# First layer's queries and keys: three matmuls of 256 columns per weight block against one of 512 and one of 256

## The chip, the core and the metric

The kernel runs on one core of a Trainium2 chip. The time is that of one execution on the device, in microseconds (us), as the median of several runs. TensorE multiplies matrices into the banks of PSUM, VectorE and ScalarE do elementwise work, GpSimd a few small things, and SyncE starts the transfers from memory. The profile calls TensorE's matmuls PE and its weight loads PEld, VectorE DVE, ScalarE ACT, GpSimd POOL and SyncE SP.

## What is computed

Two layers of an encoder over 256 tokens with 1024 features, in float32. The first layer mixes tokens in two ways at once: eight heads of attention over a neighbourhood on a grid, and eight heads of attention over compressed latents. Both start from one input projection and end in one output projection. The second layer has three groups of dilated windows. An MLP with a squared ReLU follows each. This is the part that the change touches:

```python
def even_mixer(xn, w_in, rpb, q_norm, w_uq, kv_norm, w_ukv, w_o, cos_r, sin_r):
    hcat = xn @ w_in
    o0 = 3 * NA_WIDTH                      # 1536: queries, keys and values of 8 heads of 64
    a_qkv = hcat[..., :o0].reshape(b, s, 3, NA_HEADS, HEAD_DIM)
    out_a = neighbourhood_attention(a_qkv[:, :, 0], a_qkv[:, :, 1], a_qkv[:, :, 2], rpb)
    c_q = rms_norm(hcat[..., o0:o1], q_norm)
    c_kv = rms_norm(hcat[..., o1:o2], kv_norm)
    ...
    out_b = dense_attention(q, k, v, (MLA_NOPE + MLA_ROPE) ** -0.5)
    return jnp.concatenate([out_a, out_b], axis=-1) @ w_o

for layer in range(DEPTH):
    xn = rms_norm(x, norm_mix[layer])
    x = x + even_mixer(xn, ...) if layer % 2 == 0 else x + odd_mixer(xn, ...)
    x = x + sq_relu_mlp(rms_norm(x, norm_mlp[layer]), mlp_w1[layer], mlp_w2[layer])
```

## The kernel before

**Two parts of every number.** The matmuls take a shortened form of float32. To keep precision, each operand is held as two tensors: the rounded value ("high") and what is left of it ("low"). A product is the sum of three matmuls: high times high, high times low, low times high. The helper `mm3` (L185 to L187) does that, always into the same part of one bank. The helper `split` makes the two parts: ScalarE rounds (L181), VectorE subtracts (L182).

**The tokens.** `pair_tile` holds both parts of the normalised tokens beside each other, as 8 row blocks of 2 times 256 columns: `xh` is the high part of a block, `xl` the low part, `xp` both as one stretch of 512 columns. The MLP (L370, L371) and the second layer's queries and keys (L867, L868) use `xp`: one matmul of 512 columns puts the high weight times both parts into the two halves of a bank, a second of 256 adds the low weight times the high part to the first half, and when the bank is emptied the halves are added.

**The weights.** They come from memory in chunks of 2048 columns, in the order of a list. `weight()` hands out the next chunk and sends for later ones: loads run four chunks ahead, splits two.

**The first layer's row of work.** First comes a part whose order is written out by hand (latents and values, L533 and around). Then come four chunks of queries and keys, one for each pair of heads (`qk_steps`, L621 and below). A chunk is four steps: feature half f = 0 (queries) and 1 (keys), each in two halves of four row blocks, with one `mm3` per row block. Both feature halves go into one bank, half and half. After the last step VectorE multiplies the bank by `both` (L636), which holds the tokens' scales, and `split` gives `qk_h` and `qk_l`, from which the scores of two heads are made.

The list `main` holds these steps of chunks 1 to 3, then the latent projections (`uq_steps`, `ukv_steps`), then three quarters of the output projection. Between them the attention is spread by estimated costs: for each of 16 items a score (L194 for the neighbourhood, `mm3` for the latents), its softmax on VectorE and ScalarE (L728 to L736), four transposes of its probabilities (L743), their copy to SBUF (L745) and the mixture with the values (L757). That is only the order in which the program is written. Outside the part with a hand-written order, the framework's scheduler makes each engine's order from it, by priorities and estimates of its own.

**Banks.** PSUM has eight banks here, four under the name `w` and four under `acc`, handed out in turn. Chunk 0 of queries and keys uses `w`, the others `acc`, as do the mixtures of the first six items and the latent projections. Scores and transposes use `w`. A bank is free again once everything that reads it is done.

Of the kernel before, what the change touches and what calls it, by code (L numbers as in the profile page):

```python
# [19 lines left out]
ALU = mybir.AluOpType  # L20
# [5 lines left out]
KT = D // P  # L26
T = 256
# [19 lines left out]
def trunk(ctx, tc, a, out):  # L47
    nc = tc.nc
# [8 lines left out]
    def scratch(shape, name):  # L57

        n = int(np.prod(shape))
        v = work.tile([P, 512], F32, tag="scratch", name=name, bufs=12)[:, :n]  # L60
        if len(shape) == 2:
            v = v.rearrange("p (a b) -> p a b", b=shape[1])
        return v

    def pair_tile():


        z = act.tile([P, KT, 2, T], F32R, tag="pair", name="pair", bufs=1)
        return z[:, :, 0, :], z[:, :, 1, :], z
# [7 lines left out]
    def bank(tag):  # L77
        return ps.tile([P, 512], F32, tag=tag, name=tag)
# [5 lines left out]
    def load_x(k, n=1):  # L84
        c = slice(4 * KT + k * T if k else 0, 4 * KT + (k + n) * T)
        nc.sync.dma_start(gx[:, c], a["gx"][:, c])
# [56 lines left out]
    def load_weight(edges=None, earlier=lambda i: None):  # L143
        j = state["loaded"]
        src, n = specs[j]
        raw = wraw.tile([P, WCH], F32, tag="raw", name="raw")
        edges = edges or (0, n)
        for i, c in enumerate(slice(*e) for e in zip(edges, edges[1:])):
            earlier(i)
            nc.sync.dma_start(raw[:, c], src[:, c])  # L150
        parts[j] = [raw, None, None]
        state["loaded"] = j + 1
# [13 lines left out]
    def prefetch(loads, splits):  # L166
        while state["loaded"] < min(loads, len(specs)):
            load_weight()
        while state["split"] < min(splits, len(specs)) * WPARTS:
            split_piece()  # L170

    def weight():

        j = state["used"]
        prefetch(j + 1, j + 1)
        prefetch(j + LOAD_AHEAD, j + SPLIT_AHEAD)
        state["used"] = j + 1
        return parts.pop(j)[1:]

    def split(hi, lo, src, eng=None):  # L180
        a = nc.scalar.copy(hi, src).ins  # L181
        return a, (eng or nc.vector).tensor_tensor(lo, src, hi.bitcast(F32), op=ALU.subtract).ins  # L182

    def mm3(o, sh, sl, mh, ml, first, last):
        nc.tensor.matmul(o, sh, mh, start=first, stop=False)  # L185
        nc.tensor.matmul(o, sh, ml, start=False, stop=False)  # L186
        nc.tensor.matmul(o, sl, mh, start=False, stop=last)  # L187
# [27 lines left out]
    def two(z):  # L215
        return z.rearrange("p (f n) -> p f n", f=2)
# [68 lines left out]
    def hand_over(accs, last, n):  # L285

        xT, s = pair_tile(), sum_tile()
        for b in range(4):
            last[b]()
            with tc.high_priority(NORM_PRIO):  # L290
                join(b, accs[b], n, xT)
        return xT, s

    def hand_over_tokens(accs, last, n, scale):

        xT, s = pair_tile(), sum_tile()
        ys = {}

        def leave(h, t):
            last(h, t)  # L300
            acc, sc = accs[2 * t + h], column(scale, t)
            with tc.high_priority(NORM_PRIO):
                y = ys[h, t] = scratch([512], "y")
                nc.scalar.activation(y[:, 0:T], acc[:, 0:T], AF.Copy, scale=sc)
                nc.vector.tensor_scalar(y[:, T:2 * T], acc[:, T:2 * T], sc, None, ALU.mult)

        def turn(h):
            with tc.high_priority(NORM_PRIO):
                for b in range(2):
                    pt = bank("w")  # L310
                    for k in range(2):
                        for t in range(NT):
                            c = (2 * b + k) * P
                            nc.tensor.transpose(pt[:, k * T + t * P:k * T + (t + 1) * P], ys[h, t][:, c:c + P], ident)
                    join(2 * h + b, pt, n, xT)

        leave(0, 0)
        leave(0, 1)
        leave(1, 0)
        turn(0)  # L320
        leave(1, 1)
        turn(1)
        return xT, s
# [166 lines left out]


    def even(ep):
        xT = xh, xl, _ = pair_tile()
        load_weight((0, 416, CV, CV + 416, 2 * CV), lambda i: load_x(i // 2) if i % 2 == 0 else None)
        load_weight((0, CV, 2 * CV), lambda i: load_x(2, 2) if i == 0 else None)
        load_weight((0, 2 * 416, 4 * 416), lambda i: load_x(4 + 2 * i, 2))
        both = ep.tile([P, 2, T], F32, name="both")
# [125 lines left out]
        def qk_steps(c):  # L623
            hold = {}

            def step(f, half):
                if not hold:
                    hold["w"], hold["p"] = weight(), bank("acc" if c else "w")
                (wh, wl), pq = hold["w"], hold["p"]
                for k in range(4 * half, 4 * half + 4):  # L630
                    ws = slice(k * 256 + f * P, k * 256 + f * P + P)
                    mm3(pq[:, f * T:(f + 1) * T], wh[:, ws], wl[:, ws], xh[:, k, :], xl[:, k, :], k == 0, k == KT - 1)
                if f == 1 and half == 1:
                    th, tl = (ep.tile([P, 2, T], F32R, tag=n, name=n, bufs=2) for n in ("qk_h", "qk_l"))
                    q32 = scratch([2, T], "q32")
                    nc.vector.tensor_tensor(q32, pq.rearrange("p (f n) -> p f n", f=2), both, op=ALU.mult)  # L636
                    split(th, tl, q32)
                    qk[c] = th, tl

            return [lambda f=f, h=h: step(f, h) for f in range(2) for h in range(2)]  # L640
# [368 lines left out]
    def phase(name, fn, *args):  # L1009
        with tc.tile_pool(name=name, bufs=1, reuse_waits="tile") as pool:  # L1010
            return fn(pool, *args)

    accs, last = phase("even", even)
    xT, s = hand_over(accs, last, 1)
    accs, last, scale = phase("mlp0", mlp_between, xT, s)
    xT, s = hand_over_tokens(accs, last, 2, scale)
    accs, last = phase("odd", odd, xT, s)
    xT, s = hand_over(accs, last, 3)
# [95 lines left out]
```

## Time and profile before

| | us |
|---|---|
| median of 3 runs | 747.87 |
| lowest, highest | 747.73, 748.14 |
| the profiled execution | 748.65 |
| its span, first to last instruction | 746.9 |
| first matmul of the queries and keys | 26.79 |
| first matmul of the latent projections | 58.36 |
| first matmul of the first MLP | 114.39 |

The three last rows are places in the span. All rows of a profile that follow come from the one profiled execution. A row of a timeline has the start and the length in us, then the engine, the line of the kernel, the operation, the tile written and the tiles read, the shapes and a count. Where a row has a bracket, the engine stood idle before it for that long, and the arrow names what ended the idle time. The granted clock of TensorE was 0.997 of the full one on average.

### The profile page before, as it was taken

The page shows a single profiled execution, that of the slowest core. Times are in us where ns is not written, and L with a number is a line of the kernel's source. Part 1 is how long each engine was busy: PE and PEld are TensorE (multiplying, and loading weights), DVE is VectorE, ACT ScalarE, POOL GpSimd, SP SyncE. Part 2 cuts the span into 40 slices and gives each one's busy share as a digit, 9 for nine tenths or more (in the row PEclk, how much of TensorE's full clock was granted, in tenths as well). Part 3 has the DMA queues.
Part 4 walks back from the last instruction along what each step waited for, and adds up shares of the span by engine and source line. Part 5 has one row for each costly group of instructions (what it writes and reads, how often), then busy time and mean ns, then how long its engine had stood idle before and what let it go on. Part 6 is the DMA issues. An engine that isn't in the chain of part 4 may idle for free.

```text
span 746.9 us, 12279 instructions
## 1 busy us (share of the span) xinstructions
PE 739.0 (99%) x4635; PEld 646.4 (87%) x4635; DVE 544.2 (73%) x1137; ACT 484.8 (65%) x1075; POOL 8.7 (1%) x20
## 2 busy tenths in 40 slices
PE   9999999999999999999999999999999999999996
PEld 6998998888888888889899899998998888888885
DVE  6778858766566666997888788888858765665664
ACT  6788967554554555677786877867856554554551
POOL 0100000000000001000000000000000000000000
PEclk9999999999999999999999999999999999999998
DMA  8763334464555545554645636445545555545501
GB/s 282 317 255 114 114 113 170 171 225 173 179 211 177 186 172 165 200 183 165 208 141 178 223 122 215 165 162 198 203 165 176 190 198 197 186 183 187 193 15 56
DMA packets 25163, 133.19 MB, mean 178 GB/s; under 512 B 3728, under 2 KB 4752, under 8 KB 12304
## 3 DMA queue, kind: packets, MB, share of 16 engines
q1 hardware_dynamic: 24960, 132.15, 50.1%
q8 instruction: 36, 0.59, 0.3%
q10 hardware_dynamic: 144, 0.26, 0.1%
q14 instruction: 23, 0.19, 0.1%
HBM read 127.16 MB, written 1.05 MB: 172 GB/s over the span
## 4 chain that ended last, share of the span: by engine, by line
PE 93%; DMA 3%; DVE 1%; issue 1%; SPq 1%; ACT 1%; POOL 0%; POOLq 0%; ACTq 0%
PE w L370 16%; PE acc L185 14%; PE acc L187 13%; PE acc L186 13%; PE acc L867 12%; PE w L371 8%; PE acc L868 6%; PE w L194 1%; PE w L945 1%; PE w L925 1%; PE w L743 1%; DMA gx<-in_gx 1%; DMA bias<-in_rpb 1%; DMA raw<-in_w_v 1%; PE w L757 1%
## 5 line engine op out<-in xcount | busy, mean ns | idle before, releaser
L182 DVE TENSOR_TENSOR wlo<-raw,whi 128x512 fp32r<-128x512 f32 (+3 forms) x487 | 306.6, 664 | 135.1 <-ACT whi L181 134.4
L181 ACT CAST whi<-raw 128x512 fp32r<-128x512 f32 (+3 forms) x487 | 264.3, 601 | 171.3 <-PE w L370 62.3
L370 PE MATMUL w<-pair,whi 128*128 128x512 f32 x512 | 182.2, 397 | 0.0
L371 PE MATMUL w<-pair,wlo 128*128 128x256 f32 x512 | 143.9, 281 | 0.0
L867 PE MATMUL acc<-pair,whi 128*128 128x512 f32 x384 | 139.4, 403 | 0.0
L370 PEld LDWEIGHTS w<-pair,whi 128*128 128x128 f32 x512 | 96.2, 188 | 23.2
L868 PE MATMUL acc<-pair,wlo 128*128 128x256 f32 x384 | 108.1, 282 | 0.0
L185 PE MATMUL acc<-whi,hh 128*128 128x512 f32 x250 | 98.1, 392 | 0.0
L187 PE MATMUL acc<-whi,hl 128*128 128x512 f32 x250 | 97.7, 391 | 0.0
L186 PE MATMUL acc<-wlo,hh 128*128 128x512 f32 x250 | 97.7, 391 | 0.0
L371 PEld LDWEIGHTS w<-pair,wlo 128*128 128x128 f32 x512 | 96.1, 188 | 0.9
L867 PEld LDWEIGHTS acc<-pair,whi 128*128 128x128 f32 x384 | 72.2, 188 | 16.2
L868 PEld LDWEIGHTS acc<-pair,wlo 128*128 128x128 f32 x384 | 72.2, 188 | 0.2 <-issue 0.2
L187 PEld LDWEIGHTS acc<-whi,hl 128*128 128x128 f32 x250 | 47.0, 188 | 9.9
L185 PEld LDWEIGHTS acc<-whi,hh 128*128 128x128 f32 x250 | 47.0, 188 | 9.8
L186 PEld LDWEIGHTS acc<-wlo,hh 128*128 128x128 f32 x250 | 47.0, 188 | 8.9
L185 PE MATMUL acc<-whi,pair 128*128 128x384 f32 x128 | 43.8, 342 | 0.0
L187 PE MATMUL acc<-whi,pair 128*128 128x384 f32 x128 | 43.1, 337 | 0.0
L186 PE MATMUL acc<-wlo,pair 128*128 128x384 f32 x128 | 43.1, 337 | 0.0
L374 ACT COPY side<-w 128x256 f32<-128x256 f32 x64 | 23.7, 370 | 22.1 <-PE w L371 22.1
L375 DVE TENSOR_TENSOR u<-w,side 128x256 f32<-128x256 f32 x64 | 27.0, 421 | 3.8 <-ACT side L374 3.0
L181 ACT CAST hh<-hsq 128x512 fp32r<-128x512 f32 x32 | 19.9, 621 | 10.2 <-DVE hsq L377 10.2
(215 smaller groups left out, 1112.3 us busy)
## 6 DMA issues: line engine op xcount, KB each, us to landing
raw<-in_w SPq DMA_DIRECT2D x64, 1024.0 KB, 4.8
raw<-in_w_oqk SPq DMA_DIRECT2D x24, 1024.0 KB, 5.0
raw<-in_w_ov SPq DMA_DIRECT2D x16, 768.0 KB, 4.4
raw<-in_w_qk SPq DMA_DIRECT2D x4, 1024.0 KB, 8.9
raw<-in_w_oe SPq DMA_DIRECT2D x4, 1024.0 KB, 5.2
sw<-qk SPq DMA_DIRECT2D x64, 64.0 KB, 2.4
raw<-in_w_oo SPq DMA_DIRECT2D x4, 1024.0 KB, 5.1
bias<-in_rpb SPq DMA_DIRECT2D x8, 256.0 KB, 4.2
```

What stands on the lines that cost most here:

```text
L181: a = nc.scalar.copy(hi, src).ins
L182: return a, (eng or nc.vector).tensor_tensor(lo, src, hi.bitcast(F32), op=ALU.subtract).ins
L185: nc.tensor.matmul(o, sh, mh, start=first, stop=False)
L186: nc.tensor.matmul(o, sh, ml, start=False, stop=False)
L187: nc.tensor.matmul(o, sl, mh, start=False, stop=last)
L194: nc.tensor.matmul(o[j], y[pb, 0, ts], z[pb, 1, :], start=n == 0, stop=n == 2)
L370: nc.tensor.matmul(two(pu[f]), w[0][:, c], xT[2][:, k], start=k == 0, stop=False)
L371: nc.tensor.matmul(pu[f][:, 0:T], w[1][:, c], xT[0][:, k, :], start=False, stop=k == KT - 1)
L374: nc.scalar.copy(side[:, f], pu[f][:, T:2 * T])
L375: nc.vector.tensor_tensor(u[:, f], pu[f][:, 0:T], side[:, f], op=ALU.add)
L867: nc.tensor.matmul(two(pq), wh[:, ws], xp[:, k], start=k == 0, stop=False)
L868: nc.tensor.matmul(pq[:, 0:T], wl[:, ws], xh[:, k, :], start=False, stop=k == KT - 1)
```

## The change

In `qk_steps` the three matmuls of 256 columns give way to one of 512 columns (the high weight with both parts of the tokens) and one of 256 (the low weight with the high part). The 512 columns fill a bank, so each feature half has a bank of its own: two per chunk instead of one. When a feature half is complete, VectorE adds the halves of its bank into `q32` with one TENSOR_REDUCE; after the second one `q32` is multiplied by `both` in place and split as before.

```diff
-        xT = xh, xl, _ = pair_tile()
+        xT = xh, xl, xp = pair_tile()
...
                 if not hold:
-                    hold["w"], hold["p"] = weight(), bank("acc" if c else "w")
-                (wh, wl), pq = hold["w"], hold["p"]
+                    hold["w"], hold["q"] = weight(), scratch([2, T], "q32")
+                if half == 0:
+                    hold["p"] = bank("acc" if c else "w")
+                (wh, wl), pq, q32 = hold["w"], hold["p"], hold["q"]
                 for k in range(4 * half, 4 * half + 4):
                     ws = slice(k * 256 + f * P, k * 256 + f * P + P)
-                    mm3(pq[:, f * T:(f + 1) * T], wh[:, ws], wl[:, ws], xh[:, k, :], xl[:, k, :], k == 0, k == KT - 1)
+                    nc.tensor.matmul(two(pq), wh[:, ws], xp[:, k], start=k == 0, stop=False)
+                    nc.tensor.matmul(pq[:, 0:T], wl[:, ws], xh[:, k, :], start=False, stop=k == KT - 1)
+                if half == 1:
+                    nc.vector.tensor_reduce(q32[:, f], pq.rearrange("p (h n) -> p n h", h=2), axis=mybir.AxisListType.X, op=ALU.add)
                 if f == 1 and half == 1:
...
-                    q32 = scratch([2, T], "q32")
-                    nc.vector.tensor_tensor(q32, pq.rearrange("p (f n) -> p f n", f=2), both, op=ALU.mult)
+                    nc.vector.tensor_tensor(q32, q32, both, op=ALU.mult)
                     split(th, tl, q32)
```

In the changed kernel the two matmuls are L636 and L637, the sum is L639, the multiplication L642, and every line below is six higher than before (the transposes L749, the mixtures L763, the score minimum L734).

The built orders of the two kernels differ from the first query-key matmul to the end of the first layer. Three places follow.

On TensorE, around the score of the third item (its L194 rows; `pp` are probabilities, `qk_h` and `qk_l` the parts of a chunk's queries and keys; "x2" are the two heads), before:

```order
L187 MATMUL acc<-pair,wlo 128x256
L743 MATMUL w<-ident,pp 128x128 x4
L194 MATMUL w<-qk_h 128x256 x2
L194 MATMUL w<-qk_l,qk_h 128x256 x2
L194 MATMUL w<-qk_h,qk_l 128x256 x2
L185 MATMUL acc<-pair,whi 128x256
```

And at the same place in the changed kernel:

```order
L636 MATMUL acc<-pair,whi 128x512
L749 MATMUL w<-ident,pp 128x128 x2
L194 MATMUL w<-qk_h 128x256
L749 MATMUL w<-ident,pp 128x128 x2
L194 MATMUL w<-qk_l,qk_h 128x256
L194 MATMUL w<-qk_h,qk_l 128x256
L637 MATMUL acc<-pair,wlo 128x256
L636 MATMUL acc<-pair,whi 128x512
L637 MATMUL acc<-pair,wlo 128x256
L194 MATMUL w<-qk_h 128x256
L194 MATMUL w<-qk_l,qk_h 128x256
L194 MATMUL w<-qk_h,qk_l 128x256
```

The four transposes and the score stood whole; now the two heads' matmuls stand apart, with transposes and three projections between them. The first item's score is cut in a similar way, by four projections behind its first pass.

On TensorE in the output projection (the rows that read `oah` and `oal`), at a mixture (L757, of `pts` with the values `vml`), before:

```order
L187 MATMUL acc<-oah,wlo 128x256
L743 MATMUL w<-ident,pp 128x128 x4
L757 MATMUL w<-pts,vml 64x128 x4
L185 MATMUL acc<-oah,whi 128x256
```

And in the changed kernel:

```order
L185 MATMUL acc<-oah,whi 128x256
L749 MATMUL w<-ident,pp 128x128 x2
L763 MATMUL w<-pts,vml 64x128
L749 MATMUL w<-ident,pp 128x128 x2
L763 MATMUL w<-pts,vml 64x128 x3
L187 MATMUL acc<-oah,wlo 128x256
```

The transposes and the mixture are cut into each other. That pattern stood at one mixture before and stands at three now.

On VectorE, from the second latent split to the split of chunk 1 (`cl` is a latent's low part, `sn` and `mn` are a score and its minimum), before:

```order
L182 TENSOR_TENSOR cl<-w,ch 128x3x128
L636 TENSOR_TENSOR q_527<-acc,both 128x512
L728 ISA sn,mn<-w,bias 128x256
L728 ISA mn 128x1
L728 ISA sn,mn<-w,bias 128x256
L728 ISA mn 128x1
L182 TENSOR_TENSOR qk_l<-q_527,qk_h 128x512
```

And in the changed kernel:

```order
L182 TENSOR_TENSOR cl<-w,ch 128x3x128
L639 TENSOR_REDUCE q_457<-acc 128x256 x2
L734 ISA sn,mn<-w,bias 128x256
L734 ISA mn 128x1
L642 TENSOR_TENSOR q_457<-q_457,both 128x512
L734 ISA sn,mn<-w,bias 128x256
L734 ISA mn 128x1
L182 TENSOR_TENSOR wlo<-raw,whi 128x512
L182 TENSOR_TENSOR qk_l<-q_457,qk_h 128x512
```

The first minimum stood behind one multiplication and stands behind two sums; the multiplication stands between the two heads' minima.

## The prediction

> **What bounds the kernel now.** I read the page's busy shares and its chain of work first, then the busy time of the two stretches that the change can touch, then who waited for whom on TensorE there.
>
> ```profile
> PE 739.0 (99%) x4635; PEld 646.4 (87%) x4635; DVE 544.2 (73%) x1137; ACT 484.8 (65%) x1075; POOL 8.7 (1%) x20
> ...
> PE 93%; DMA 3%; DVE 1%; issue 1%; SPq 1%; ACT 1%; POOL 0%; POOLq 0%; ACTq 0%
> ```
>
> ```profile
> 26.79:58.36 31.57, 31.39 (x280) 28.92 (x278) 25.19 (x80) 27.08 (x74) 2.14 (x4) 1.00 0.68 251
> 58.36:114.39 56.03, 56.03 (x474) 49.75 (x473) 44.38 (x136) 46.45 (x129) 0.88 (x3) 1.00 0.32 112
> ```
>
> ```profile
> PE w L556 <- DVE cn L548: 0.2, 1, 0.2
> ```
>
> The first stretch runs from the first query-key matmul to the first matmul of the latent projections, the second from there to the first matmul of the MLP. The columns are length, then busy time of TensorE matmuls, weight loads, VectorE, ScalarE and GpSimd, then granted clock, DMA share and GB/s. TensorE is busy for 31.39 of 31.57 us and 56.03 of 56.03, at a granted clock of 1.00, and its one listed wait is 0.2 us. The chain is TensorE's for 93%. So a microsecond more or less in TensorE's row of instructions moves the end by about as much, and VectorE (25.19 of 31.57) matters only where it makes TensorE wait. Because matmul ends are modelled and overlap, I price TensorE from start to start, not by the busy time of one.
>
> **The matmuls themselves.** Before, each of 64 steps (4 weights, 2 feature halves, 8 row blocks) issues three matmuls of 256 columns; after, one of 512 and one of 256. Both are 768 columns. The trace has both forms, on the same moving tile and with weights of the same shape.
>
> ```profile
> 26.79 0.28 PE L185 MATMUL w<-pair,whi 128*128 128x256 f32 x1
> ...
> 30.89 0.61 PE L265 MATMUL w<-diag,mean 128*128 128x128 f32 x4
> ```
>
> ```profile
> 149.77 0.40 PE L370 MATMUL w<-pair,whi 128*128 128x512 f32 x1
> ...
> 154.36 0.39 PE L185 MATMUL acc<-whi,hh 128*128 128x512 f32 x1
> 154.59 0.39 PE L186 MATMUL acc<-wlo,hh 128*128 128x512 f32 x1
> ```
>
> Between the first two rows stand 36 matmuls of 256 (12 steps): (30.89 − 26.79)/36 = 0.114 us each, 0.342 a step. Between 149.77 and 154.36 the MLP does 13 pairs of the new form (26 matmuls): 4.59/13 = 0.353 a step. The new form is 0.0114 us slower, times 64: **+0.7 us**. What it saves, 64 weight loads, is hidden: they lie beside matmuls already.
>
> The Trainium skill, "TensorE: Matmul & The Clock Gate", section "Back-to-back issue gap", gives a warm gap of N/2.4 + 2.5 ns between matmuls standing alone. By it three of 256 take 327.5 ns and a pair 325.0, so the change would gain 64 × 2.5 ns = 0.16 us as an estimate. The trace disagrees: 342 against 353 ns; I go by the trace.
>
> **The order of the row on TensorE.** The built order shows that the change also moves what stands between the projections. Scores (L194), transposes of probabilities (L743) and mixtures (L757) are cut into pieces at places where they stood whole.
>
> ```profile
> 39.11 0.28 PE L187 MATMUL acc<-pair,wlo 128*128 128x256 f32 x1
> 39.31 0.38 PE L194 MATMUL w<-qk_h 64*128 64x256 f32 x2
> 39.54 0.28 PE L194 MATMUL w<-qk_l,qk_h 64*128 64x256 f32 x2
> 39.66 0.28 PE L194 MATMUL w<-qk_h,qk_l 64*128 64x256 f32 x2
> 39.86 0.38 PE L185 MATMUL acc<-pair,whi 128*128 128x256 f32 x1
> 40.09 0.28 PE L186 MATMUL acc<-pair,whi 128*128 128x256 f32 x1
> ```
>
> Going over to a score and back costs: the last projection before it takes 39.31 − 39.11 = 0.20 instead of 0.11, the first behind it 0.23. So one more cut through a score by projections costs 0.20 on the projections, and some 0.1 on the score, whose piece ends with a gap of 0.20 (39.66 to 39.86) where 0.12 stands between its passes. The first score is cut once: **+0.3 us**.
>
> ```profile
> 82.53 0.38 PE L743 MATMUL w<-ident,pp 128*128 128x128 f32 x2
> 82.84 0.43 PE L757 MATMUL w<-pts,vml 128*64 128x128 f32 x2
> 83.20 0.44 PE L743 MATMUL w<-ident,pp 128*128 128x128 f32 x2
> 83.57 0.65 PE L757 MATMUL w<-pts,vml 128*64 128x128 f32 x6
> 84.15 0.39 PE L185 MATMUL w<-kh,qh 96*128 96x256 f32 x1
> ```
>
> ```profile
> 89.91 0.60 PE L743 MATMUL w<-ident,pp 128*128 128x128 f32 x4
> 90.44 0.66 PE L757 MATMUL w<-pts,vml 128*64 128x128 f32 x8
> 91.03 0.39 PE L185 MATMUL acc<-oah,whi 128*128 128x256 f32 x1
> ```
>
> The same four transposes and one mixture take 84.15 − 82.53 = 1.62 us cut into each other and 91.03 − 89.91 = 1.12 whole: a cut of this kind costs 0.50. The third score stood whole behind four transposes; after, its two heads, which ran side by side (rows with x2), stand apart, cut by two transposes and by three projections. By the two rows above that is 0.5 + 0.3: **+0.8 us**. In the output projection the pattern "two transposes, a piece of a mixture, two transposes, the rest" stands three times where it stood once: **+1.0 us**. A mixture in the second stretch is cut 3 to 1 by four transposes, and elsewhere single projections stand between pairs of transposes, while other transposes lose the gap that they have in front of a score (44.84 to 45.37: 0.53) against a projection (55.31 to 55.67: 0.36).
>
> ```profile
> 44.84 0.60 PE L743 MATMUL w<-ident,pp 128*128 128x128 f32 x4
> 45.37 0.39 PE L194 MATMUL w<-qk_h 64*128 64x256 f32 x2
> ...
> 55.31 0.60 PE L743 MATMUL w<-ident,pp 128*128 128x128 f32 x4
> 55.67 0.37 PE L185 MATMUL acc<-pair,whi 128*128 128x256 f32 x1
> ```
>
> These go both ways by 0.17 or so apiece: between −0.3 and +0.3, taken as **0**.
>
> **The idle that goes.** TensorE stands still once in the first stretch, for the normalised latent rows:
>
> ```profile
> 34.31 0.28 PE L187 MATMUL acc<-pair,wlo 128*128 128x256 f32 x1
> 34.77 0.52 PE L556 MATMUL w<-ident,cn 128*128 128x128 f32 x3 [0.18 <-DVE cn L548]
> ```
>
> The gap is 0.46 where 0.11 is normal. After, these transposes stand behind 20.5 steps of 0.353 instead of 20 of 0.342, about 0.4 us later, and VectorE's order up to them is unchanged: the idle of 0.35 us is filled, **−0.35**. What is late next is the first score.
>
> **VectorE.** Eight sums over a bank are added. The odd layer has the same operation:
>
> ```profile
> L876 DVE TENSOR_REDUCE qk<-acc 128x256 f32<-128x512 f32 x24 | 16.5, 686 | 5.1 <-PE acc L868 4.9
> ...
> L636 DVE TENSOR_TENSOR q<-acc,both 128x512 f32<-128x512 f32 x3 | 2.1, 692 | 1.5 <-PE acc L187 1.5
> ```
>
> ```profile
> 310.82 0.69 DVE L876 TENSOR_REDUCE qk<-acc 128x256 f32<-128x512 f32 x1
> 311.43 0.68 DVE L182 TENSOR_TENSOR wlo<-raw,whi 128x512 fp32r<-128x512 f32 x1
> ```
>
> From start to start one takes 0.61 us, eight 4.9; the multiplication by `both` stays, now from SBUF, and keeps its 0.69. VectorE's 25.19 us become about 30.1 in a stretch of some 33: 91%. Behind a sum stand, in VectorE's row, the score minimum (L728), the split of q and k (L182 to qk_l) and weight splits; TensorE waits for these through the softmax and for the split. The first minimum stands behind two sums now, 1.2 us. The cover is the distance from a score to the transposes of its probabilities: the score ends at 39.86, the transposes begin at 44.84, 5.0 us. And VectorE at 91% is already seen without harm:
>
> ```profile
> 58.00:76.00 18.00, 18.00 (x142) 14.92 (x140) 16.46 (x56) 16.42 (x49) 0.88 (x3) 1.00 0.24 82
> ```
>
> 16.46 of 18 us on VectorE, and TensorE busy through all 18. So new waits cost between 0 (this row) and 4.9 us (every sum in TensorE's way, no cover). I take **+0.3**, near this row, about the one idle that TensorE shows before. Banks: each weight now takes two in turn instead of one; a bank comes round after four, steps of 2.8 us, and the sum that frees it takes 0.61.
>
> **Sum.** 0.7 + 0.3 + 0.8 + 1.0 + 0 − 0.35 + 0.3 = +2.8 us (2.75). The profiled execution took 748.65 us (span 746.9, 1.75 around it), 0.78 above the median shown, 747.87. Against itself: 751.4; against the median: **750.7 us**. About 0.2% (1.5 us) is what a measurement here can tell from no change; this is 0.37%.
>
> **Rivals.**
> 1. The cuts cost nothing, since the scheduler put them where TensorE would have stood still. Then 0.7 is left, or 0.35 with the idle filled: 748.6 or 748.2, 748.4 as the middle, within 0.2%. Against it: the second stretch has no idle to fill (56.03 of 56.03). Chance 0.13.
> 2. On the other side, not slower: the pair of matmuls runs at the rate that 512 columns reach in the MLP's down projection, 154.59 − 154.36 = 0.23 us, and a 256 at 0.114. Then a step costs 0.342 as before, the cuts are free as in rival 1, and the filled idle is all that is left: 747.5 us. This decides if the pair takes under 0.345. The Trainium skill's formula, given above, would take 0.16 more off. Against it: 13 pairs in a row at 0.353. Chance 0.09.
> 3. VectorE becomes the bound: from the point where its backlog exceeds the 5.0 us of cover, each sum passes into TensorE's row. With half of the eight, 2.4 us more: 752.9; with all, 755.3. For it: 91% busy and a row in a fixed order. Against: the row at 58 to 76. Chance 0.15.
>
> **How the numbers follow.** The forecast, with TensorE's row priced as above, has 0.63. Its own range is 749.4 to 752.2, from the bounds of the small terms and of the waits up to 1.5. For 8 in 10 it reaches down to rival 1 and up to the first price of rival 3: 748.4 to 752.9. Slower by over 0.2% (above 749.4): 0.63 + 0.15, less 0.01 for the forecast's lower edge, 0.77. The rest, 0.23, is rivals 1 and 2 and that edge: 0.20 within 0.2%, and 0.03 faster, for a rival 2 in which more idle goes than the rows show.
>
> **What would show it.** In the profile after, a projection step of 0.353 us from start to start in the first layer; the first MLP matmul (L370 before) at about 117.1 instead of 114.39, and the same distance from there to the end; TensorE still busy throughout; VectorE's sums at 0.61 with no TensorE wait on them over 0.3 us. Wrong would be a step of 0.342, a first MLP matmul before 115.5 (the cuts are free), or rows of TensorE waiting for the sums or for the minimum behind them (rival 3).

## The result and the profile after

| | before | after |
|---|---|---|
| median, us | 747.9 (4 runs, 747.73 to 748.14) | 756.55 (4 runs, 755.71 to 757.25) |
| ratio | | 1.0115, 95% interval 1.0102 to 1.0128 |
| profiled execution / its span | 748.65 / 746.9 | 755.71 / 753.9 |
| first query-key matmul | 26.79 | 26.80 |
| first matmul of the latent projections | 58.36 | 63.64 |
| first matmul of the first MLP | 114.39 | 121.32 |

The kernel is 8.65 us slower by the medians, 7.06 by the two profiled executions (a high one of before, the lowest of after). From the first MLP matmul to the end of the span they take 632.5 and 632.6 us. All of the loss lies in the two stretches that the change touches: 5.27 us in the first and 1.65 in the second.

The page's busy shares and its chain, of the kernel after:

```profile
PE 744.0 (99%) x4571; PEld 646.6 (86%) x4571; DVE 549.9 (73%) x1146; ACT 484.5 (64%) x1074; POOL 8.7 (1%) x20
...
PE 97%; issue 1%; ACT 1%; DVE 1%; POOL 0%; POOLq 0%
```

The two stretches after, with the same columns as before (length, then busy time of TensorE matmuls, weight loads, VectorE, ScalarE and GpSimd, granted clock, DMA share, GB/s), and who waited for whom on TensorE:

```profile
26.80:63.64 36.84, 34.62 (x216) 27.67 (x214) 29.48 (x85) 26.50 (x73) 2.05 (x3) 0.95 0.57 200
63.64:121.32 57.68, 57.68 (x474) 50.51 (x473) 45.18 (x137) 46.39 (x129) 0.88 (x3) 1.00 0.33 115
```

```profile
PE acc L763 <- ACT pts L751: 2.2, 1, 2.2
```

The page hides the event: 99% busy, 97% of the chain. The stretch shows it: TensorE is busy for 34.62 of 36.84 us, and the clock granted over the stretch is 0.95. The only listed wait is for ScalarE, not for VectorE: the first mixture waits 2.2 us for the copy of the transposed probabilities.

TensorE's row of the kernel after, at the pair steps, at that wait and behind it, and at the cut mixtures of the second stretch:

```profile
26.80 0.39 PE L636 MATMUL w<-pair,whi 128*128 128x512 f32 x1
...
31.02 0.60 PE L265 MATMUL w<-diag,mean 128*128 128x128 f32 x4
...
48.64 0.28 PE L194 MATMUL w<-qk_h,qk_l 64*128 64x256 f32 x1
51.14 0.94 PE L763 MATMUL acc<-pts,vna 128*64 128x128 f32 x8 [2.22 <-ACT pts L751]
52.00 0.80 PE L636 MATMUL acc<-pair,whi 128*128 128x512 f32 x1
52.60 0.41 PE L637 MATMUL acc<-pair,wlo 128*128 128x256 f32 x1
...
57.91 0.66 PE L763 MATMUL acc<-pts,vna 128*64 128x128 f32 x8
58.50 0.39 PE L194 MATMUL w<-qk_h 64*128 64x256 f32 x2
...
73.04 0.65 PE L763 MATMUL acc<-pts,vna 128*64 128x128 f32 x6
73.62 0.66 PE L749 MATMUL w<-ident,pp 128*128 128x128 f32 x4
74.21 0.43 PE L763 MATMUL acc<-pts,vna 128*64 128x128 f32 x2
74.57 0.45 PE L185 MATMUL acc<-whi,ch 128*128 128x384 f32 x1
...
89.12 0.38 PE L749 MATMUL w<-ident,pp 128*128 128x128 f32 x2
...
90.75 0.39 PE L185 MATMUL w<-kh,qh 96*128 96x256 f32 x1
```

Twelve pairs take 31.02 − 26.80 = 4.22, or 0.352 a step. A mixture takes 52.00 − 51.14 = 0.86 right behind the wait, but 58.50 − 57.91 = 0.59 later: the clock is low there.

```profile
48.85:51.14 2.29, 0.07 (x2) 0.00 (x1) 1.67 (x7) 2.29 (x8) 0.00 (x0) 1.00 0.90 368
51.14:54.31 3.17, 3.17 (x17) 2.56 (x18) 1.36 (x6) 2.82 (x9) 0.00 (x0) 0.54 0.40 101
```

Two windows of the kernel after: the wait, and the 3.17 us behind it at a clock of 0.54. Cut finer, the clock is 1.00 until 51.37, 0.23 us after TensorE has gone on, then 0.50 for 3.41 us, and 1.00 again from 54.78.

Why was ScalarE late? Its row of the kernel after, and the same place in the kernel before:

```profile
44.29 0.91 ACT L742 ACTIVATE pp<-pp,rz 128x256 f32<-128x256 f32 x2 [0.50 <-DVE rz L740]
48.29 1.34 ACT L181 CAST whi<-raw 128x384 fp32r<-128x384 f32 x3 [3.09 <-PE acc L636]
49.53 0.50 ACT L739 ACTIVATE pp<-sn,mn 128x256 f32<-128x256 f32 x1
...
50.52 0.56 ACT L751 COPY pts<-w 128x512 f32<-128x512 f32 x1
```

```profile
47.27 0.49 ACT L733 ACTIVATE pp<-sn,mn 128x256 f32<-128x256 f32 x1
...
47.76 0.50 ACT L181 CAST whi<-raw 128x384 fp32r<-128x384 f32 x1
48.16 0.58 ACT L745 COPY pts<-w 128x512 f32<-128x512 f32 x1
```

After, three casts of the latent-query weight (128x384) stand at the head of ScalarE's row. The idle time ahead of them ends with a query-key matmul (`<-PE acc L636`): they write into a weight buffer that a chunk of queries and keys still uses. So ScalarE stands idle for 3.09 us with the second item's exponentials and the first item's copy queued behind it. Before, one such cast stood there, behind the exponentials and without idle. No line of the diff is about it: the scheduler's new order put the casts ahead.

### The profile page after: what moved, and what is told of

Its sections match the earlier page's. It is cut to its first block, busy times and chain, and to the rows that moved or that the text cites. A ratio compares the mean times of both kernels' runs of the same rounds, so it can differ in the third digit from the quotient of the medians.

```text
span 753.9 us, 12154 instructions
## 1 busy us (share of the span) xinstructions
PE 744.0 (99%) x4571; PEld 646.6 (86%) x4571; DVE 549.9 (73%) x1146; ACT 484.5 (64%) x1074; POOL 8.7 (1%) x20
## 4 chain that ended last, share of the span: by engine, by line
PE 97%; issue 1%; ACT 1%; DVE 1%; POOL 0%; POOLq 0%
PE w L370 16%; PE acc L185 13%; PE acc L187 13%; PE acc L186 13%; PE acc L873 12%; PE w L371 8%; PE acc L874 6%; PE acc L533 3%; PE acc L636 2%; PE w L194 1%; PE w L951 1%; PE w L931 1%; PE w L749 1%; PE w L763 1%; PE acc L637 1%
```

## The experiments

Two theories went in. **A**: the sums are covered, and the loss lies in the order that the scheduler built, in the casts at the head of ScalarE's row and the cuts in TensorE's. **B**: the eight sums on VectorE are what TensorE waits for. **C**, the smaller rival, puts the loss on the pair of matmuls. The kernel before was run beside each batch: 747.96, 748.01 and 748.00 us.

**1. The casts on GpSimd.** The kernel after; the four pieces of this one weight are rounded on GpSimd.

```diff
-        return split(hi, lo, raw, eng)
+        return split(hi, lo, raw, eng, nc.gpsimd.tensor_copy if j == 9 else nc.scalar.copy)
...
```

> The changed kernel with the four roundings of the latent query weight (the 128x384 casts) done by GpSimd instead of ScalarE; nothing else is edited. Theory A (the row of ScalarE): these casts wait for the buffer that chunk 2 of queries and keys still uses, and stand ahead of the second item's softmax and the first item's copy; TensorE then stands still for 2.3 us and runs at a clock of 0.54 for 3.2 us after it. Without them in the row: no idle of TensorE over 0.5 us at the first mixture, clock 1.00 there, and about 3.8 us less than the changed kernel, 752 us. Theory B (VectorE's eight sums, 4.9 us, are what TensorE waits for): the idle stays at 1.5 us or more, and the time is within 1 us of the changed kernel, 755.5 or more.

Measured: 752.49 us (752.18 to 752.57), ratio 1.006 [1.0045, 1.0075]. In ScalarE's row the copy now stands at 47.13, and on TensorE the mixture follows without the wait:

```profile
47.13 0.56 ACT L751 COPY pts<-w 128x512 f32<-128x512 f32 x1
```

```profile
47.90 0.65 PE L763 MATMUL acc<-pts,vna 128*64 128x128 f32 x6
49.28 0.44 PE L749 MATMUL w<-ident,pp 128*128 128x128 f32 x2 [0.72 <-ACT pp L742]
```

So the casts' place costs 756.55 − 752.49 = 4.1 us, with the rest of the order built anew too. Inside the mixture an idle time of 0.72 us is left, where at most 0.5 was expected: its second transposes wait for the second item's probabilities. ScalarE waits for VectorE's reciprocal for these, and that (at 48.53) stands behind one of the new sums (at 47.47) and weight splits. The other 4.5 us over the kernel before stay; where they lie is taken up behind run 11.

**2. The wait kept, TensorE kept busy in it.** Ten matmuls on constants are put into the bank of the first mixture, ahead of it; the mixture starts the bank anew.

```diff
             pvo = bank("acc" if n < 6 else "w")
+            for _ in range(10 if n == 0 else 0):
+                nc.tensor.matmul(pvo, warm[:, 0:P], warm, start=True, stop=True)
```

> The changed kernel with ten matmuls of 512 columns on constants in front of the first mixture on TensorE, which fill its idle time; their results are overwritten. The first mixture should begin at about 51 us of the span as in the changed kernel. If the low clock after the idle time (0.54 for 3.2 us) comes from the idle time itself, the clock stays at 1.00 there and the time is 1.3 to 1.8 us less: 754 to 755. If the low clock has another cause, it stays, and the time is that of the changed kernel or 0.5 more.

Measured: 753.97 us (753.89 to 754.09), ratio 1.008 [1.0065, 1.0095]. ScalarE's row has the same 3.09 us of idle time and the same three casts ahead of the copy, and the mixture still comes late, 24.56 us after the first query-key matmul (24.34 in the kernel after). But it runs at full speed:

```profile
50.97 0.66 PE L765 MATMUL acc<-pts,vna 128*64 128x128 f32 x8
51.56 0.39 PE L637 MATMUL acc<-pair,wlo 128*128 128x256 f32 x1
```

```profile
50.97:54.00 3.03, 3.03 (x27) 2.34 (x26) 2.35 (x9) 3.03 (x10) 0.00 (x0) 1.00 0.59 124
```

The mixture takes 0.59 and the clock stays at 1.00. So the idle time brings the low clock, and of the 4.1 us the clock is 2.6 by the medians, or 1.8 by the profiled spans (753.92 − 752.10), the wait itself the rest. Half speed for 3.41 us loses 1.7 us, which fits the spans. That the medians differ by more is not explained: the other three executions of the kernel after left no trace, and their mean clocks are lower (0.994 to 0.995) than the profiled one's (0.996).

**3. No sums, order free.** The sum is replaced by a copy of the bank's first half (0.42 us instead of 0.68).

```diff
-    nc.vector.tensor_reduce(q32[:, f], pq.rearrange("p (h n) -> p n h", h=2), axis=mybir.AxisListType.X, op=ALU.add)
+    nc.vector.tensor_copy(q32[:, f], pq[:, 0:T])
```

> The changed kernel with each sum of a bank's halves replaced by a copy of its first half (0.4 us instead of 0.6), which leaves out the product of the high weights with the low part of the tokens in the queries and keys. The scheduler then puts the copy of the first item's probabilities ahead of the latent casts. Theory A: no long idle, low clock gone, TensorE's order still cut: 751 to 752, the same as e1 within 0.7. Theory B: the sums are the cost, so this is 2 us or more faster than e1 and near 749.

Measured: 752.1 us (751.39 to 752.41), ratio 1.0054 [1.0039, 1.0069], with no wait on TensorE at all. That is the time of run 1 within 0.4, as A has it, and not B's 749: in an order that the scheduler builds freely, shorter work on VectorE gained nothing clear. The run isn't a clean one, since the eight copies still stand where the sums stood, and the scheduler built yet another order, with its own cuts.

**4. Three matmuls of 256, two banks, sums kept.**

```diff
-    nc.tensor.matmul(two(pq), wh[:, ws], xp[:, k], start=k == 0, stop=False)
+    nc.tensor.matmul(pq[:, 0:T], wh[:, ws], xh[:, k, :], start=k == 0, stop=False)
+    nc.tensor.matmul(pq[:, T:2 * T], wh[:, ws], xl[:, k, :], start=False, stop=False)
```

> The changed kernel with the product done as three matmuls of 256 columns again (the second into the second half of the bank); two banks per chunk and the eight sums stay. Here one latent cast stands ahead of the second item's softmax. Theory A: 0.7 us less for the form, and an idle time of 1 to 2 us at the first mixture with a lower clock behind it: 753 to 755. Theory C (the pair form is most of the cost): within 1 us of the kernel before, 747 to 749.

Measured: 754.37 us (753.16 to 755.93), ratio 1.0093 [1.0076, 1.0109]; the first mixture waits 1.4 us for the same copy. The time and the wait are as A put them; the lower clock that A had behind the wait is not in the trace (1.00). Without the pair form most of the loss is still there: C falls.

In the next runs TensorE's order is held to the order in which the program is written, from the first query-key chunk to the end of the output projection, so that kernels can be compared piece by piece.

**5 to 7. One order: the kernel before; with two banks and sums; with the pair too.**

```diff
+        with tc.manual_schedule(engines={ENG.PE}):
             first = qk_steps(0)
...
             main.insert(1, (0, turn_c[1]))
```

Run 5 has this in the kernel before, run 6 in the kernel of run 4, run 7 in the kernel after.

> The kernel before, with TensorE's row in the first layer held to the order in which the program is written, from the first query-key matmul to the output projection; the other engines' rows stay the scheduler's. This is the reference for e6, e7 and e8, in which TensorE's row has the same groups in the same order. Expected within 1 us of the kernel before, 747 to 749.

> e5 with two banks per chunk, the second matmul of 256 into the second half, and VectorE's eight sums: the whole change but for the pair form, and with TensorE's order held. Theory A (sums are covered, the cost is in the order): within 0.6 us of e5. Theory B (VectorE's 4.9 us are the cost): 2 us or more above e5.

> The changed kernel with TensorE's row held to the program's order: no score or mixture is cut, and the latent casts stand behind the second item's softmax on ScalarE. Against e6 only the matmul form differs: plus 0.7 us (64 steps of 0.353 instead of 0.342). Theory A: 0.7 to 1.3 above e5, about 749, without the long idle. If the cuts cost nothing (rival 1 of the prediction), it equals e1 less nothing: 752.

Measured: run 5 748.86 us (ratio 1.0011 [1.0002, 1.0021]), run 6 751.7 (1.0048 [1.0033, 1.0063]), run 7 752.16 (1.0054 [1.0039, 1.0069]). The second banks with their sums cost 751.70 − 748.86 = **2.8 us**, the pair of matmuls **0.5** more, with nothing moved in TensorE's row. With the order held, B's number for run 6 is met (2 us or more) and A's are missed: 0.6 us for run 6, about 749 for run 7. Run 7's 752 is also what its expectation gave for cuts that cost nothing; but the rows have waits in place of the cuts. Waits of TensorE in run 5, then in run 6:

```profile
PE w L649 <- DVE qtok L521: 0.7, 1, 0.7
PE w L649 <- ACT kh L181: 0.3, 1, 0.3
```

```profile
PE w L656 <- DVE qtok L521: 1.5, 2, 0.8
PE w L194 <- DVE mn L735: 0.5, 1, 0.5
PE w L750 <- ACT pts L752: 0.5, 1, 0.5
PE w L194 <- DVE qk_l L182: 0.4, 1, 0.4
```

1.0 us of waits becomes 2.9. From start to start a wait costs more than the idle time listed for it. The first in time, at the first score of run 6:

```profile
38.30 0.39 PE L194 MATMUL w<-qk_h 64*128 64x256 f32 x2
39.12 0.39 PE L194 MATMUL w<-qk_l,qk_h 64*128 64x256 f32 x2 [0.44 <-DVE qk_l L182]
```

From one pass to the next it is 0.82 us here and 38.81 − 38.59 = 0.22 in run 5, so 0.60 for a listed 0.44. The chain behind it, VectorE's rows of run 5, then of run 6:

```profile
34.28 0.68 DVE L636 TENSOR_TENSOR q<-w,both 128x512 f32<-128x512 f32 x1
...
36.19 0.68 DVE L182 TENSOR_TENSOR qk_l<-q,qk_h 128x512 fp32r<-128x512 f32 x1
...
39.30 0.41 DVE L728 CUSTOM_DVE_ANT_0 sn<-w,bias 128x256 f32<-128x256 f32 x1
```

```profile
34.68 0.68 DVE L640 TENSOR_REDUCE q<-w 128x256 f32<-128x512 f32 x1
...
35.38 0.68 DVE L640 TENSOR_REDUCE q<-w 128x256 f32<-128x512 f32 x1
...
36.58 0.68 DVE L643 TENSOR_TENSOR q<-q,both 128x512 f32<-128x512 f32 x1
...
38.39 0.68 DVE L182 TENSOR_TENSOR qk_l<-q,qk_h 128x512 fp32r<-128x512 f32 x1
...
39.46 1.27 DVE L640 TENSOR_REDUCE q<-acc 128x256 f32<-128x512 f32 x2
40.65 0.41 DVE L735 CUSTOM_DVE_ANT_0 sn<-w,bias 128x256 f32<-128x256 f32 x1
```

From the first step on the bank to the start of `qk_l` it is 1.91 us without the sums and 3.71 with them. Of the 1.80 more, 1.20 are the two sums; 0.60 is a weight split that stands behind `qk_l` in run 5 and ahead of it in run 6. `qk_l` is ready at about 39.07 in run 6, and the second pass of TensorE's first score, which reads it, starts at 39.12. The next chunk's two sums (39.46) then stand ahead of the first score's minimum: that starts 40.65 − 26.06 = 14.59 us after the first query-key matmul, instead of 39.30 − 26.42 = 12.88. The third score, the transposes and the latent queries are late behind it.

**8. Run 7 with the casts on GpSimd.**

> e7 with the latent casts on GpSimd as in e1. Theory A: since they no longer stand in front of anything in e7, this changes nothing: within 0.5 us of e7. If these casts on ScalarE cost time by themselves, it is 1 us or more below e7.

Measured: 752.06 us, ratio 1.0051 [1.0034, 1.0068], the same as run 7. With TensorE's row in written order the casts do not stand in the way, so the 4.1 us belong to the order that was built, not to ScalarE's work on the casts as such.

**9 and 10. Run 7 without sums; run 7 with half of each sum on ScalarE.** Run 9 multiplies the banks' first halves straight into `q32` (`p0` is the bank of the queries) and so leaves out the high weights times the low tokens, here as in run 3; run 10 copies the second half on ScalarE.

```diff
...
-    nc.vector.tensor_tensor(q32, q32, both, op=ALU.mult)
+    nc.vector.tensor_tensor(q32[:, 0], hold["p0"][:, 0:T], both[:, 0, :], op=ALU.mult)
+    nc.vector.tensor_tensor(q32[:, 1], pq[:, 0:T], both[:, 1, :], op=ALU.mult)
```

```diff
-    nc.vector.tensor_reduce(q32[:, f], pq.rearrange("p (h n) -> p n h", h=2), axis=mybir.AxisListType.X, op=ALU.add)
+    side = scratch([T], "side")
+    nc.scalar.copy(side, pq[:, T:2 * T])
+    nc.vector.tensor_tensor(q32[:, f], pq[:, 0:T], side, op=ALU.add)
```

> The changed kernel with TensorE's order held as written, and without the eight sums: the first halves of the two banks are multiplied by the token scales straight into q32, in two pieces of 256 columns instead of one of 512. Left out of the computation: the high weight times the low tokens in queries and keys. Theory B (the sums stand in the chain from a chunk's last matmul to its score, and later work of VectorE behind them): what is left over the kernel before in written order (748.86) is the pair form, 0.5 by the seventh run, so 749.3, 748.9 to 749.9, and the first score no later than 0.2 us against that kernel. Rival (two banks per chunk, or the changed order of banks, costs whatever VectorE does): 751 or more.

> The changed kernel in written order, with each sum shared: ScalarE copies the second half of the bank, VectorE adds 256 columns of it to the first half. VectorE's eight operations get shorter, but a copy on ScalarE stands ahead of each of them. If the length of the chain behind a chunk's last matmul counts (theory B): 751.9 to 752.8, no better than the 752.16 with the sums. If VectorE's load counts, so that some 0.25 us saved eight times comes back: 750 to 751.

Measured: run 9 749.71 us (749.51 to 750.4), ratio 1.0024 [1.0014, 1.0034]; run 10 751.13 (750.9 to 751.34), ratio 1.0042 [1.0028, 1.0057]. Run 9 is where B put it: with the sums go 752.16 − 749.71 = 2.45 us. Its first score starts 12.46 us after the first query-key matmul against 12.17 in run 5, 0.29 later where 0.2 was allowed; the 32 pair steps ahead of it, at 0.0114 each, are 0.36. Run 10 met neither number. The first stretch of run 7, then of run 10, tells where it gained:

```profile
26.23:59.84 33.61, 32.70 (x215) 26.22 (x213) 28.92 (x86) 27.30 (x75) 2.27 (x3) 1.00 0.66 236
```

```profile
26.50:59.18 32.68, 32.05 (x216) 26.18 (x214) 26.43 (x82) 28.53 (x80) 2.12 (x3) 1.00 0.66 239
```

VectorE is busy for 2.5 us less and TensorE's stretch gets 0.9 shorter. The first score of run 10 still waits, 0.29 for `qk_h` and 0.34 for `qk_l`; the waits of the third score (0.55 in run 7) and of the transposes (0.49) are gone. So the trace has both readings, each at its place: at the first score the length of the chain counts, behind it the place in VectorE's queue.

**11. The kernel before with the casts on GpSimd**, the edit of run 1.

> The kernel before with the rounding of the four pieces of the latent-query weight on GpSimd, as in the first run on the changed kernel. In the kernel before ScalarE's rounding does not stand ahead of the softmax, and TensorE waits nowhere: 747.9 within 0.3, whatever the theory; a gain of over 1 us would say that ScalarE's order costs something before the change too, and that part of the first run's gain is no part of the change.

Measured: 747.98 us (747.57 to 748.53), ratio 1.0001 [0.9991, 1.001]. The casts cost nothing before the change, so run 1's gain repairs damage that came with it. No version here beats the kernel before: the change without any sum (run 9) is still 0.85 us above the kernel before in the same order.

**Where the time lies on TensorE.** The kernel before and run 11 have the same row of instructions on TensorE, and so have runs 7 to 10. The table adds up TensorE's time between the first query-key matmul and the first matmul of the MLP, in us, each matmul from its start to the start of the next; waits are inside.

| | run 11 (the row of before) | run 1 | run 3 | run 5 | run 7 | run 9 |
|---|---|---|---|---|---|---|
| query-key projections | 23.41 | 24.41 | 25.10 | 23.41 | 24.13 | 23.96 |
| scores (L194) | 4.39 | 5.35 | 5.68 | 4.39 | 5.92 | 4.41 |
| transposes of probabilities | 7.40 | 8.04 | 7.44 | 7.66 | 8.40 | 8.03 |
| mixtures | 9.76 | 11.98 | 10.47 | 9.40 | 9.40 | 9.40 |
| all else | 42.22 | 42.18 | 42.38 | 43.30 | 43.97 | 43.23 |
| sum | 87.19 | 91.97 | 91.07 | 88.16 | 91.81 | 89.03 |

In the free orders of runs 1 and 3 the loss is in the projections, scores, transposes and mixtures, which are cut into each other. Without the one wait of run 1 (0.72) and about 0.7 for the pair, the cuts cost 3.4 us in run 1 and 3.2 in run 3, which waits nowhere. In the held order the mixtures are whole (9.40 in all three), and the loss is where TensorE waits. So the two kinds of order lose alike by the sum, and not by the same thing. That the scheduler made the cuts because of the sums is not shown: run 3 has cuts of the same price without the sums.

## Why the prediction was wrong

The direction was right; 750.7 us was 5.9 too low, and the measured time lies beyond the upper end of the range. The first MLP matmul came at 121.32 instead of about 117.1, with the same distance from there to the end, as forecast. The step that failed is the one on new waits: **"So new waits cost between 0 (this row) and 4.9 us … I take +0.3"**. It counted only waits for VectorE, and the sum had no term for ScalarE at all. In the kernel after TensorE has no listed wait for VectorE; it waits 2.2 us for ScalarE, and the low clock follows. Point by point:

- **What the sum had no term for.** ScalarE's row was not read, since the diff gives ScalarE nothing to do. The order that was built put three casts ahead of work that TensorE waits for: 4.1 us (run 1), almost half of the loss, about half of it through the clock (run 2). "TensorE still busy throughout" was the line that showed it wrong.
- **The pair of matmuls, +0.7.** Right: 0.352 a step where 0.353 was forecast, and 0.5 us from run 6 to run 7, where some of it falls into waits.
- **The cuts, +0.3, +0.8, +1.0 and 0.** Too small: 2.1 in all, where the table gives 3.4 in run 1 and 3.2 in run 3. The pattern in the output projection costs 90.75 − 89.12 = 1.63 against 1.12 whole, 0.51 a time, as priced, and stands three times where it stood once: +1.0. What was put at 0 was not: the mixture cut by four transposes at 73.04 takes 74.57 − 73.04 = 1.53 and adds 0.41. These two make most of the second stretch's 1.65.
- **The idle that goes, −0.35.** Those transposes carry no wait in the profile after, but that is not the change's doing. Run 11 has the row of the kernel before, the same order on VectorE up to that place, and no wait there. The idle time belonged to the one profiled execution, which was 0.78 above the median, so it should not have been taken off against the median.
- **The +0.3 for VectorE.** Run 1 has 0.72 of such waits, through the reciprocal. Where TensorE's order is held, the sums cost 2.5 us (run 9) and the banks with them 2.8 (run 6), inside the bounds; the value in them rested on a chain that was not the shortest. The prediction took the way from a score to the transposes of its probabilities, 5.0 us, as the cover. A shorter one was there to be read, from a chunk's last matmul over the multiplication and `qk_l` to that chunk's score. VectorE's rows of the kernel before:

```profile
35.69 0.69 DVE L636 TENSOR_TENSOR q<-w,both 128x512 f32<-128x512 f32 x1
...
37.59 0.70 DVE L182 TENSOR_TENSOR qk_l<-q,qk_h 128x512 fp32r<-128x512 f32 x1
```

`qk_l` was ready at 38.29, and the second pass of the first score read it at 39.54: a cover of 1.25 us. Two sums at 0.60 leave next to nothing of it, and the weight split of 0.60 that moved ahead in run 6 is then too much. "What is late next is the first score" named the place without this measure. Nor does VectorE at 91% without harm say anything about another chain: run 6 waits with VectorE busy for 28.82 of 33.18 us, 87%.

- **The rivals.** The third, VectorE as the bound, has a first price of 2.4 us, which is near what the sums cost with the order held. That its 752.9 is within 0.5 of run 1, the kernel without the casts in the way, is luck: run 1 loses by cuts, and the sign that was given for this rival, TensorE waiting for the sums or the minimum behind them, is not in the profile after. Rivals 1 and 2 are refuted by the cuts' price and the step of 0.352.

The account in medians, with the order held: 748.0 for the kernel before, plus 0.85 for the written order (run 5), 2.84 for banks and sums (run 6), 0.46 for the pair (run 7): 752.16. The order that was built for the kernel after costs about as much (752.49) once the casts are out of the way, by cuts instead of waits, and 4.1 us more as it is.

Two things stay open. Run 9 shows that all but 0.85 us over run 5 goes with the sums; the table puts 0.55 of that on the projections, which are pairs, and 0.37 on transposes, the cause of which was not separated. And why the scheduler cut the rows and put the casts ahead was not found; that the casts wait there for a buffer is in the trace, and that moving them brings back the time is shown.

## What to carry to other kernels

When a scheduler builds the order, read the rows of all engines, those that the diff doesn't touch too: one instruction at the head of a queue that waits for a buffer holds up everything behind it, for 3.09 us here. When work is added to an engine off the path, look for the shortest chain through it, from the matmul that feeds it to the next matmul that needs its result, and measure that slack in the row; the busy share did not tell it here. The one idle time of TensorE over 2 us cost about twice its length, wait and low clock together. And before an idle time of one profiled execution is taken off a sum, see if a second execution has it.

## What the runs showed of the hardware

An idle time of 2.2 us was enough to bring the granted clock down to 0.50, for 3.41 us. The clock fell 0.23 us after TensorE had gone on, not in the idle time itself. The Trainium skill, "TensorE: Matmul & The Clock Gate", section "Why this matters for your kernels", says to keep idle gaps between bursts of matmuls under about 3 us. The trace here has a clock drop at 2.2 us, so the rule is too generous for this case; with ten matmuls on constants in the gap the drop did not occur.

The spread of the runs may go with it, which is not shown. The kernel of run 4, with 1.4 us of idle, ran from 753.16 us at a mean clock of 0.998 to 755.93 at 0.995, a spread of 2.8 us; all 18 runs of the kernel before beside runs 9 to 11 lie within 1.2. That an idle time of 1.4 us costs the clock in some executions and not in others fits this, but only the fastest of those executions left a trace, and in it the clock stays at 1.00 behind the idle time.
